# The down projection of a decoder layer as seven products of quadrants, with act split in two parts ahead and read back from DRAM

## The chip, the core and the metric

The kernel runs on one core of one Trainium2 chip. The metric is the device time of one execution in microseconds. The kernel before was run three times on the chip; the median counts, and one more execution was profiled.

## The reference

One decoder layer over 512 tokens of width 2048: an attention block with two groups of heads, then a gated feed-forward block of width 5632. All is float32. What the change touches is the last matrix product and what feeds it:

```python
h = rmsnorm(x, g_pre_ffn[l]) * (1.0 + sc_f) + sh_f
f = (jax.nn.silu(h @ w_gate[l]) * (h @ w_up[l])) @ w_down[l]
x = x + gt_f * rmsnorm(f, g_post_ffn[l])
```

Below, `act` is the 512 x 5632 matrix silu(gate) * up, and the down projection is act @ w_down, 512 x 5632 by 5632 x 2048. gt_f is a gate that comes from another product (w_ada), 2048 numbers, one for each output column.

## The kernel before

**Arithmetic.** A float32 product is made of three products of float32r parts: each factor is split in hi (a rounded copy, ACT) and lo (the rest, DVE), and `mm_x` (L281) issues hi*hi, lo*hi and hi*lo (L282 to L284) into one PSUM bank, 128 rows by 512 columns each. The weights are the moving operand, 512 columns; act or h is the stationary one, 128 columns.

**Steps.** The program is a list of steps. A step has one weight tile of 128 x 1024 (512 KB), which is two chunks of K by 512 columns. The main loop runs the steps in order and looks LA = 2 steps ahead: `do_hi` (L1533) lets ACT write w_hi of the step after next in the middle of a step, `do_lo` (L1542) lets DVE write w_lo at its end. Both have three buffers, so w_hi of step i+2 waits until TensorE is through with step i-1. Around this, events hang on a step: `start_ev`, `pe_ev`, `post_ev` (before do_lo), `post_end` (after it). Every engine works through its own instructions in the order in which this loop writes them, so the order of the events is the order on each engine. A transfer that SP starts waits in SP's order too, for a free buffer or for what it writes.

**Gate and up.** Steps F0 to F1 (32 steps) make the first group of 512 columns plainly. From F1 there are ten groups g of 28 steps each, with seven products of quadrants (Winograd's form: m1, P, Q, Y2, R, m2, T, four steps each, 12 matmuls a step). h's quadrants and their four sums E1 to E4 lie in SBUF in two parts; the sums of E are made during F0 to F1 (`e_sums` L1230, on DVE, with ACT's copy in the same event; `e_lo`). The sums of the weight quadrants are made in place: `w_load` (L1374) has SP fetch raw tiles; `w_sums` (L1386) adds to them by POOL's accumulating DMAs (P += B11 and P += B21 and R += B22) or by DVE (P += B22). A group's results are copied and combined out of PSUM (`s_copy`, `s_comb`), gated (`s_act1`, `s_act2a`, `s_act2b`) and transposed by TensorE (`act_tr`, L1250). ACT copies the transposed pieces to a stage buffer and its own queue writes them to a DRAM tile `act2d`, in float32. Five stage pieces of 128 x 1024 are shared among all this.

**Down.** Steps D0 on, 88 steps: four groups cg of 512 output columns, 22 steps of K each, 24 matmuls a step (four row blocks tb, two chunks of K, three part products). For every step SP fetches one weight tile and one act tile (512 KB each), ACT makes w_hi and the hi part of act (acthl, L967), DVE makes w_lo and the lo part of act (L971). So act is fetched and split four times over. 32 of the steps also carry a dot for gt_f on DVE (`ada_dot`, L226, a fetched 128 x 1024 tile each).

**End.** When a group cg is done, ACT squares its four banks with a running sum (L1475) and DVE multiplies them by the gain (L1479). The last three steps are held back and run row block by row block; after each block follow square, gain, `rstd` (L1141, L1145, and a power on POOL, L1146) and the outputs (L1488), which SP and ACT write to DRAM.

## Time and profile before

| what | value |
|---|---|
| runs | 2246.09, 2248.93, 2249.97 us; median 2248.93 |
| profiled execution, its own time | 2250.6 us |
| its span, first to last instruction | 2248.8 us |
| mean granted TensorE clock | 0.995 |
| one gate and up group (28 steps) | 78.33 us |
| down projection, first to last matmul start | 1759.1 to 2239.5 us |
| last matmul's start to the end | 9.3 us |
| DMA over the span | 524.02 MB, 233 GB/s |

A profile line of a group names line, engine, operation, output<-inputs, shape and count, then busy time, mean ns of one, and the idle time before it with what ended it. PE is TensorE's matmuls, PEld its weight loads. Matmuls overlap: the duration of one is longer than the distance from one to the next, so a rate is read from starts. A stretch of the windows view has busy time and count for PE, PEld, DVE, ACT and POOL, then the granted clock, the busy share of the 16 DMA engines, and GB/s.

### The profile page before, as it was taken

To read this page: it belongs to the slowest core of one execution; us is meant where nothing else is said; L and a number is where in the kernel's file an instruction comes from. 1 tells how busy PE (TensorE), PEld (TensorE's weight loads), DVE (VectorE), ACT (ScalarE), POOL (GpSimd) and SP (SyncE) were. 2 spreads that over 40 slices of the span, in tenths; PEclk is the share of its full clock that TensorE was granted. 3 is DMA by queue.
4 is the path that set the end of the run, shared out by engine and by line. 5 is a ranking of instruction groups with operands and counts; after the bars stand their busy time and mean duration, and the time that the engine had idled before them with its cause. 6 is when DMAs were issued, how large, how long until landed. Compare 5 with 4: busy or idle time off the path is not lost.

```text
span 2248.8 us, 27045 instructions
## 1 busy us (share of the span) xinstructions
PE 2214.3 (98%) x10012; PEld 1807.1 (80%) x10012; DVE 1471.7 (65%) x2117; ACT 1030.5 (46%) x1507; POOL 142.7 (6%) x156
## 2 busy tenths in 40 slices
PE   7999999999999999999999999999999999999998
PEld 6888777778887888777888888888888888888886
DVE  6987878776767676765566556556655666544445
ACT  5443344444435565544445445444544433343432
POOL 0000000000001000010111111011111000000000
PEclk9999999999999999999999999999999999999999
DMA  9786544556678787788877977897797788865564
GB/s 366 298 335 216 166 144 143 157 157 203 212 247 279 254 290 255 259 266 257 236 198 222 273 201 208 260 241 202 213 273 197 252 291 289 279 196 189 198 222 178
DMA packets 147845, 524.02 MB, mean 233 GB/s; under 512 B 16353, under 2 KB 27905, under 8 KB 141313
## 3 DMA queue, kind: packets, MB, share of 16 engines
q1 hardware_dynamic: 111696, 427.11, 54.6%
q0 software_dynamic: 17280, 62.92, 14.7%
q10 hardware_dynamic: 18736, 32.27, 4.6%
q8 instruction: 78, 1.28, 0.2%
q14 instruction: 55, 0.44, 0.1%
HBM read 488.14 MB, written 25.18 MB: 228 GB/s over the span
## 4 chain that ended last, share of the span: by engine, by line
PE 90%; DVE 4%; DMA 3%; issue 1%; ACT 1%; POOL 0%; SPq 0%; ACTq 0%; DVEq 0%; POOLq 0%
PE b L283 23%; PE b L284 23%; PE b L282 23%; PE b L277 5%; PE b L279 5%; PE b L278 5%; PE b L507 2%; DMA w_lent<-in_wgu 2%; DVE w_lo L1546 1%; PE b L545 1%; PE b L529 1%; PE b L1260 1%; PE b L500 1%; ACT w_hi L1537 1%; DMA w_raw<-in_wout 1%
## 5 line engine op out<-in xcount | busy, mean ns | idle before, releaser
L1546 DVE TENSOR_TENSOR w_lo<-w_raw,w_hi 128x1024 fp32r<-128x1024 f32 x264 | 321.9, 1222 | 280.3 <-ACT w_hi L1537 280.1
L1537 ACT ACTIVATE w_hi<-w_raw 128x1024 fp32r<-128x1024 f32 x264 | 278.3, 1057 | 424.0 <-PE b L284 333.2
L1546 DVE TENSOR_TENSOR w_lo<-raw,w_hi 128x1024 fp32r<-128x1024 f32 x189 | 230.5, 1223 | 186.6 <-ACT w_hi L1537 185.7
L282 PE MATMUL b<-w_hi,h 128*128 128x512 f32 x864 | 343.5, 398 | 1.9 <-ACT w_hi L1537 1.5
L283 PE MATMUL b<-w_lo,h 128*128 128x512 f32 x864 | 339.8, 393 | 5.0 <-DVE w_lo L1546 4.0
L284 PE MATMUL b<-w_hi,h 128*128 128x512 f32 x864 | 338.2, 391 | 0.0
L1537 ACT ACTIVATE w_hi<-raw 128x1024 fp32r<-128x1024 f32 x189 | 200.1, 1060 | 256.9 <-PE b L284 190.0
L284 PE MATMUL b<-w_hi,acthl 128*128 128x512 f32 x704 | 274.0, 389 | 0.4 <-DVE acthl L971 0.4
L282 PE MATMUL b<-w_hi,acthl 128*128 128x512 f32 x704 | 274.2, 389 | 0.0
L283 PE MATMUL b<-w_lo,acthl 128*128 128x512 f32 x704 | 273.9, 389 | 0.0
L283 PE MATMUL b<-w_lo,e 128*128 128x512 f32 x640 | 249.5, 390 | 2.2 <-DVE w_lo L1546 2.2
L282 PE MATMUL b<-w_hi,e 128*128 128x512 f32 x640 | 250.0, 391 | 0.3 <-ACT w_hi L1537 0.3
L284 PE MATMUL b<-w_hi,e 128*128 128x512 f32 x640 | 249.0, 389 | 0.0
L277 PE MATMUL b<-h,w_hi 128*128 128x512 f32 x512 | 212.9, 416 | 0.2 <-ACT h L257 0.2
L278 PE MATMUL b<-h,w_hi 128*128 128x512 f32 x512 | 200.5, 392 | 3.0 <-DVE h L273 3.0
L279 PE MATMUL b<-h,w_lo 128*128 128x512 f32 x512 | 201.3, 393 | 0.0
L283 PEld LDWEIGHTS b<-w_lo,h 128*128 128x128 f32 x864 | 163.1, 189 | 45.1 <-DVE w_lo L1546 11.7
L282 PEld LDWEIGHTS b<-w_hi,h 128*128 128x128 f32 x864 | 163.0, 189 | 40.2 <-issue 3.7
L284 PEld LDWEIGHTS b<-w_hi,h 128*128 128x128 f32 x864 | 163.0, 189 | 33.8
L1546 DVE TENSOR_TENSOR w_lo<-w_lent,w_hi 128x1024 fp32r<-128x1024 f32 x91 | 111.1, 1223 | 88.0 <-ACT w_hi L1537 87.7
L1537 ACT ACTIVATE w_hi<-w_lent 128x1024 fp32r<-128x1024 f32 x91 | 96.5, 1060 | 131.0 <-PE b L284 97.3
L284 PEld LDWEIGHTS b<-w_hi,acthl 128*128 128x128 f32 x704 | 132.2, 188 | 28.4 <-DVE acthl L971 0.8
(251 smaller groups left out, 3273.6 us busy)
## 6 DMA issues: line engine op xcount, KB each, us to landing
raw<-in_wgu SPq DMA_DIRECT2D x133, 512.0 KB, 8.8
w_raw<-in_adar SPq DMA_DIRECT2D x128, 512.0 KB, 4.3
w_raw<-in_win SPq DMA_DIRECT2D x107, 512.0 KB, 5.0
actf<-act2d SPq DMA_DIRECT2D x88, 512.0 KB, 4.7
w_raw<-in_wdown SPq DMA_DIRECT2D x88, 512.0 KB, 3.5
raw<-in_wgu POOLq DMA_DIRECT2D x82, 512.0 KB, 9.5
w_lent<-in_wgu SPq DMA_DIRECT2D x67, 512.0 KB, 8.7
w_raw<-in_wout SPq DMA_DIRECT2D x64, 512.0 KB, 4.9
```

The lines of the kernel that those rows point to most:

```text
L277: pe.matmul(ps, whi, ahi, start=start, stop=False, **kw)
L278: pe.matmul(ps, whi, alo, start=False, stop=False, **kw)
L279: pe.matmul(ps, wlo, ahi, start=False, stop=stop, **kw)
L282: pe.matmul(ps, ahi, whi, start=start, stop=False, **kw)
L283: pe.matmul(ps, ahi, wlo, start=False, stop=False, **kw)
L284: pe.matmul(ps, alo, whi, start=False, stop=stop, **kw)
L500: pe.matmul(sc[:, r], qk[:, i, qs], qk[:, i + 1, :N], start=True, stop=True)
L507: pe.matmul(sc[:, :N], qk[k, 2 * m, qs], qk[k, 2 * m + 1, :N], start=True, stop=True)
L529: pe.transpose(tr[:, j, :], misc["p"][:, n % 2, 128 * j:128 * j + 128], ident)
L545: pe.matmul(h["pv"][:, qb, :], d["pt"][:, o:o + 128], v[:, j, e], start=j == 0, stop=j == qb)
L1537: act.activation(hi, raw, AF.Copy)
L1546: dve.tensor_tensor(lo, raw, hi.bitcast(F), op=OP.subtract)
```

## The change

act is cut in four quadrants, two halves of rows and two halves of K (the even and the odd chunks of 128 of each group of 512, which is one of eleven steps j). w_down is cut in two halves of columns c, and each of these in quadrants of K and of 512 columns, which the host only lays out anew. For each c there are seven products of 11 steps with 12 matmuls: m1 (A11 by B11), P, R and Y2 (sums E1, E3, E4), then Q and m2 in turn, then T. Each sums its 11 steps in two PSUM banks; Q goes on in m1's banks and T in R's. The order of the steps and their transfers is fixed by lists:

```diff
+        DB = {"X": (0, 1), "Y": (4, 5), "Z": (2, 3), "W": (6, 7)}
+        DP = {"m1": ("A11", "X"), "P": ("E1", "Y"), "R": ("E3", "Z"), "Y2": ("E4", "W"),
+              "Q": ("E2", "X"), "m2": ("A12", "Y"), "T": ("A22", "Z")}
+        DUSE = {"m1": "C", "P": "C", "Q": "C", "T": "C", "R": "B12", "Y2": "B22", "m2": "B21"}
...
+            for j in range(2, 11):
+                seq += [("m1", j + 1)] * (j < 10) + [("P", j), ("R", j), ("Y2", j)]
+            for j in range(11):
+                seq += [("Q", j), ("m2", j)]
+            seq += [("T", j) for j in range(11)]
...
+                for k in range(2):
+                    ts_ = slice(128 * tb, 128 * tb + 128)
+                    mm_x(ps, hi4[:, k, :], lo4[:, k, :], at[:, 0, k, ts_], at[:, 1, k, ts_],
+                         first and k == 0, j == 10 and k == 1, skip_group_check=True)
```

Weight tile C holds B11 first; DVE adds B12, B22 and B21 to it in turn (and B22 to B12 for R), four sums of 128 x 1024 per j and c. The loads run 7 or 8 steps ahead, the act tiles and the tiles of the gt_f dots 5 steps:

```diff
+                dloads += [(dpos[c, "m1", j] - 7, dpos[c, "m1", j] - 4, c, "C", 0, j),
+                           (dpos[c, "P", j] - 8, dpos[c, "P", j] - 5, c, "B12", 1, j),
+                           (dpos[c, "R", j] - 8, dpos[c, "R", j] - 5, c, "B22", 3, j),
+                           (dpos[c, "m2", j] - 7, dpos[c, "m2", j] - 4, c, "B21", 2, j)]
+        dloads += [(i - 5, i - 2, 2, "dot", 0, i) for i in dots]
...
+        aloads = [(i - 5, *dseq[i - D0]) for i in range(D0, NSTEP)]
```

act's quadrants and sums are made while the next gate and up group runs, split in two parts there, and written to DRAM by SP (seven tiles of 512 KB a group, where 1 MB in float32 was written by ACT's queue before). A down step fetches one such tile and splits nothing but the weights:

```diff
+        def act_parts(g, at):
+
+            post_end[at].append(lambda: act_e(g, 0))
+            post_end[at + 1].append(lambda: act_e(g, 1))
+            for n, what in enumerate(("e0", "e1", "v0", "v1")):
+                post_end[at + 2 + 3 * n].append(lambda what=what: act_hi(g, what))
+                post_end[at + 3 + 3 * n].append(lambda what=what: act_lo(g, what))
+                start_ev[at + 4 + 3 * n].append(lambda what=what: act_out(g, what))
...
+            act_parts(g, b0 + 31)
...
-                    elif k - j == 7:
-                        pool.dma_start(rawt[g, "P", j], wgu[g, 1, j], accum_op=OP.add)
+                    elif k - j == 20:
+                        dve.tensor_tensor(rawt[g, "P", j], rawt[g, "P", j], rawt[g, "B21", j], op=OP.add)
...
+            post_end[at + 1].append(lambda j=j: e_hi(j))
+            post_end[at + 2].append(lambda j=j: e_lo(j))
```

act_e is four DVE sums of 128 x 512; act_hi is a copy on ACT into a new stage piece, act_lo a subtraction on DVE, act_out two transfers (hi, then lo), after which both pieces are free again. A sixth stage piece comes from a raw buffer. In the groups, raw buffers are fewer, and the first group fetches its third P tile at step F1 - 3 instead of F1 - 6. For h's sums, ACT's copy moves one step behind DVE's sums (e_hi).

At the end, the rows 0 to 255 are complete before T; their outputs come ahead of the last two steps (NLAST = 2), which then run for the two blocks of the lower rows:

```diff
-        NLAST = 3
+        NLAST = 2
...
+        for tb in range(2):
+            for q in range(2):
+                d_out(tb, 1024 * q, 1024)
+        for tb in range(2):
+            for i in last:
+                steps[i]["mm"](*hl[i], tb)
+            d_comb(1, 2, "R", OP.add, (tb,))
+            d_sq(1, 2, (tb,))
+            rstd(HF["dss", 2 + tb], 4)
+            d_gain(1, 2, (tb,))
+            for q in range(4):
+                d_out(2 + tb, 512 * q, 512)
```

TensorE has 9063 rows in order where it had 9327. Three places on the other engines follow. First ACT in one of the steady gate and up groups, before, from the copies of a group's first product (s1) to that of its second (y1); `stage` and `stageb` are stage pieces, DMAHW a transfer that SP or ACT started:

```order
L1289 ACTIVATE stage_6928<-b_10360 128x512
L1289 ACTIVATE stage_6928<-b_10369 128x512
L1537 ACTIVATE w_hi<-raw_7418 128x1024 [waits DMASW7_49,DVE_49,PE_49]
L1537 ACTIVATE w_hi<-w_lent 128x1024 [waits DVE_49,PE_49]
L1537 ACTIVATE w_hi<-raw_7683 128x1024 [waits DVE_49,PE_49]
L1537 ACTIVATE w_hi<-raw_7418 128x1024 [waits DVE_49,PE_49,Activation_49]
L1289 ACTIVATE stage_7304<-b_10448 128x512 [waits DMAHW7_49]
L1289 ACTIVATE stage_7304<-b_10457 128x512 [waits DMAHW0_49]
```

And after, from the copy of y1 (L1343) in step 8 of a group on; L1300 is act_hi, of e1 and then v0, L1343 further down the copy of u2:

```order
L1343 ACTIVATE stage_7304<-b_9975 128x512 [waits DMAHW6_49,DVE_49,Activation_49]
L1343 ACTIVATE stage_7304<-b_9984 128x512
L1300 ACTIVATE raw_7305<-stage_6928 128x1024 [waits DMAHW7_49]
L1704 ACTIVATE w_hi<-w_lent 128x1024 [waits DVE_49,PE_49,Activation_49]
L1704 ACTIVATE w_hi<-raw_7305 128x1024 [waits DMAHW1_49,PE_49,Activation_49]
L1704 ACTIVATE w_hi<-w_lent 128x1024 [waits DMAHW2_49,DVE_49,PE_49]
L1300 ACTIVATE raw_7305<-stageb 128x1024 [waits DMAHW2_49,DVE_49,Activation_49]
L1704 ACTIVATE w_hi<-raw_7680 128x1024 [waits DMAHW3_49,PE_49,Activation_49]
L1343 ACTIVATE stage_6928<-b_9887 128x512 [waits DMAHW3_49]
L1343 ACTIVATE stage_6928<-b_9896 128x512
L1704 ACTIVATE w_hi<-w_lent 128x1024 [waits DMAHW4_49,DVE_49,PE_49]
L1704 ACTIVATE w_hi<-raw_7681 128x1024 [waits DMASW4_49,DVE_49,PE_49]
```

Between two w_hi there are now ACT's splits, and those, like the copies, wait for a transfer that frees a stage piece; before, copies of y1 waited for act2d's writes alone.

Second, DVE in the down projection, before, two steps with a dot (L228) each:

```order
L971 TENSOR_TENSOR acthl<-actf,acthl 128x1024 [waits DMAHW1_49,PE_49,Activation_49]
L228 SCALAR_TENSOR_TENSOR w_raw,red<-w_raw,silu_back 128x1024 [waits DMAHW6_49,DVE_49]
L1546 TENSOR_TENSOR w_lo<-w_raw,w_hi 128x1024 [waits DMAHW0_49,Activation_49]
L971 TENSOR_TENSOR acthl<-actf,acthl 128x1024 [waits DMAHW4_49,PE_49,Activation_49]
L228 SCALAR_TENSOR_TENSOR w_raw,red<-w_raw,silu_back 128x1024 [waits DMAHW1_49,DVE_49]
L1546 TENSOR_TENSOR w_lo<-w_raw,w_hi 128x1024 [waits DMAHW3_49,Activation_49]
```

And after, four steps of Q and m2 in the first half, where L1713 makes w_lo, L1527 sums weight tiles (rawP, rawR, stage are buffers they lie in) and L228 is a dot:

```order
L1713 TENSOR_TENSOR w_lo<-rawR_13092,w_hi 128x1024 [waits DMAHW1_49,Activation_49]
L228 SCALAR_TENSOR_TENSOR stageb,red<-stageb,silu_back 128x1024 [waits DMAHW2_49]
L1527 TENSOR_TENSOR rawR_13093<-rawR_13093,raw_7681 128x1024
L1713 TENSOR_TENSOR w_lo<-rawP_13095,w_hi 128x1024 [waits Activation_49]
L1713 TENSOR_TENSOR w_lo<-rawP_13094,w_hi 128x1024 [waits DMAHW5_49,Activation_49]
L228 SCALAR_TENSOR_TENSOR stage_7304,red<-stage_7304,silu_back 128x1024 [waits DMAHW6_49]
L1527 TENSOR_TENSOR stage_6928<-stage_6928,rawR_13092 128x1024
L1713 TENSOR_TENSOR w_lo<-w_lent,w_hi 128x1024 [waits Activation_49]
```

The subtraction for act (L971) is gone; a pair of steps with 24 matmuls has two w_lo, a sum and a dot, where a step with 24 matmuls had one w_lo, one acthl and a dot.

Third, DVE at the end, before (du is the output tile, dss its sums, gtg the gain, x the residual), the last two row blocks:

```order
L1479 TENSOR_TENSOR du_13316<-b_15484,gtg_14444 128x512 [waits Activation_49]
L1141 TENSOR_REDUCE dss<-dss 128x1
L1145 TENSOR_SCALAR dss<-dss 128x1 [waits DVE_49]
L1488 SCALAR_TENSOR_TENSOR du_13316<-du_13316,dss,x_2_16008 128x1024 [waits DMAHW7_49,Pool_49]
L1488 SCALAR_TENSOR_TENSOR du_13316<-du_13316,dss,x_2_16008 128x1024
L1479 TENSOR_TENSOR du_13318<-b_15485,gtg_14444 128x512 [waits Activation_49]
L1141 TENSOR_REDUCE dss<-dss 128x1
L1145 TENSOR_SCALAR dss<-dss 128x1 [waits DVE_49]
L1488 SCALAR_TENSOR_TENSOR du_13318<-du_13318,dss,x_3_16076 128x512 [waits DMAHW3_49,Pool_49]
L1488 SCALAR_TENSOR_TENSOR du_13318<-du_13318,dss,x_3_16076 128x512 x3
```

And after, the two blocks of the lower rows, where L1612 adds T's bank, L1630 is the gain and L1654 the output:

```order
L1612 TENSOR_TENSOR du_14070<-du_14070,b_14806 128x512 [waits PE_49]
L1152 TENSOR_REDUCE dss<-dss 128x1 [waits Activation_49]
L1156 TENSOR_SCALAR dss<-dss 128x1 [waits DVE_49]
L1630 TENSOR_TENSOR du_14070<-du_14070,gtg_15892 128x512
L1654 SCALAR_TENSOR_TENSOR du_14070<-du_14070,dss,x_2_16070 128x512 [waits DMAHW5_49,Pool_49]
L1654 SCALAR_TENSOR_TENSOR du_14070<-du_14070,dss,x_2_16070 128x512
L1654 SCALAR_TENSOR_TENSOR du_14070<-du_14070,dss,x_2_16070 128x512 [waits DVE_49]
L1654 SCALAR_TENSOR_TENSOR du_14070<-du_14070,dss,x_2_16070 128x512
L1612 TENSOR_TENSOR du_14073<-du_14073,b_14815 128x512 [waits PE_49]
L1152 TENSOR_REDUCE dss<-dss 128x1 [waits Activation_49]
L1156 TENSOR_SCALAR dss<-dss 128x1 [waits DVE_49]
L1630 TENSOR_TENSOR du_14073<-du_14073,gtg_15892 128x512
```

A block had gain, sums and outputs; it now has a combination, sums that wait for ACT's square, the gain and four outputs, and the second block's combination stands behind the first one's outputs.

More of the change, by code (lines that the diff above doesn't have):

```diff
@@ L1262, in go_v @@
             def go_v():
                 stage.add(src())
-                p = stage.get()
-                v = v3(p, 4)
-                for n in range(2):
-                    act.activation(v[:, 2 * n:2 * n + 2, :], st[n], AF.Copy)
-                    act.dma_start(act2d[2 * g + n][:, :, 256 * half:256 * half + 256], v[:, 2 * n:2 * n + 2, :])
-                stage.add(p)
-            return go_pe, go_v
+                p = actv[g, f"v{half}"] = stage.get()
+                for f in range(2):
+                    act.activation(v3(p, 4)[:, 2 * f:2 * f + 2, :], st[f], AF.Copy)
@@ new lines, in body, with d_load @@
+        dloads.sort()
+        aloads = [(i - 5, *dseq[i - D0]) for i in range(D0, NSTEP)]
+        STAGE_RAW = ("P6", "T0", "SB", "P1")
+        XTAGS = ("P1", "P4", "R2", "R8")
+        def d_load(e):
+            while aloads and aloads[0][0] <= e:
+                c, name, j = aloads[0][1:]
+                p = apool.get()
+                assert p is not None, (e, aloads[0])
+                aloads.pop(0)
+                a_of[c, name, j] = p
+                v = p[1].rearrange("p (h k t) -> p h k t", h=2, k=2)
+                sync.dma_start(v, acts[ACOMBO[DP[name][0]], j])
+                atile[c, name, j] = v.bitcast(R)
+            while dloads and dloads[0][0] <= e:
+                at, end, c, n, q, j = dloads[0]
+                p = None
+                if c == 1 and n == "C":
+                    p = rawp.get([u for u in ("raw", "R10", "R11", "P2", "P5", *STAGE_RAW) if u not in XTAGS])
+                elif c == 1:
+                    p = rawp.get(XTAGS)
+                if p is None:
+                    p = rawp.get()
+                if p is None:
+                    assert end > e, (e, dloads[0], len(apool.free))
+                    break
+                dloads.pop(0)
+                draw_of[c, n, j] = p
+                draw[c, n, j] = p[1]
+                sync.dma_start(p[1], adar[dots[j]] if n == "dot" else wds[c, q, j])
@@ L1426, in body, with d_more @@
+        def d_more():
+            rawp.add(*stage.free)
+            stage.free = []
         w1 = wsteps[0, 1, 0, 0]
@@ new lines, in d_comb, with d_c12, d_sq @@
+        def d_comb(c, q, name, op, tbs=(0, 1)):
+            for tb in tbs:
+                dve.tensor_tensor(du(c, q, tb), du(c, q, tb), bank["d", c, name, tb], op=op)
+        def d_c12(c):
+            for tb in range(2):
+                dve.tensor_tensor(du(c, 1, tb), bank["d", c, "Y2", tb], du(c, 3, tb), op=OP.add)
+        sq = {}
+        def d_sq(c, q, tbs=(0, 1)):
+            if "t" not in sq:
+                sq["t"] = U("R7", [128, 4, 512], name="sq")
+            for tb in tbs:
+                t_, cg = 2 * (q // 2) + tb, 2 * c + q % 2
+                act.activation(sq["t"][:, tb, :], du(c, q, tb), AF.Square, accum_out=HF["dss", t_][:, cg:cg + 1])
```

278 lines of the change are left out of this document (169 added, 109 removed).

## The prediction

> **What bounds the kernel now.** I read the page first, then the down projection's matmuls, then the stages by windows, last the end of the program in order of time.
>
> The page, its first section and the chain by engine:
>
> ```profile
> span 2248.8 us, 27045 instructions
> PE 2214.3 (98%) x10012; PEld 1807.1 (80%) x10012; DVE 1471.7 (65%) x2117; ACT 1030.5 (46%) x1507; POOL 142.7 (6%) x156
> ...
> PE 90%; DVE 4%; DMA 3%; issue 1%; ACT 1%; POOL 0%; SPq 0%; ACTq 0%; DVEq 0%; POOLq 0%
> ```
>
> TensorE is the bound nearly everywhere. Whatever takes matmuls away without making TensorE wait shortens the run. The price of one matmul is not its 389 ns, though, because they overlap. The rows of the tile acthl (count, duration, first and last start) and two pairs of ACT's rows (start, duration, idle before):
>
> ```profile
> L282 PE MATMUL b<-w_hi,acthl x704: 387/389/476, 1759.1 to 2239.0; 128*128 128x512 f32 x176
> ...
> L284 PE MATMUL b<-w_hi,acthl x704: 388/389/500, 1759.7 to 2239.5; 128*128 128x512 f32 x176
> ```
> ```profile
> 2190.29 1.06 ACT L1537 ACTIVATE w_hi<-w_raw 128x1024 fp32r<-128x1024 f32 x1 [3.43 <-PE b L284]
> ...
> 2195.73 1.06 ACT L1537 ACTIVATE w_hi<-w_raw 128x1024 fp32r<-128x1024 f32 x1 [3.43 <-PE b L284]
> ```
> ```profile
> 1117.83 1.06 ACT L1537 ACTIVATE w_hi<-raw 128x1024 fp32r<-128x1024 f32 x1 [1.66 <-PE b L284]
> 1120.55 1.06 ACT L1537 ACTIVATE w_hi<-w_lent 128x1024 fp32r<-128x1024 f32 x1 [1.66 <-PE b L284]
> ```
>
> In the down projection one step (24 matmuls) takes 2195.73 - 2190.29 = 5.44 us, so a matmul costs 5.44/24 = 0.2267 us. The gate and up groups already run steps of 12 matmuls: 1120.55 - 1117.83 = 2.72 us, again 0.2267 each. The stage lasts 2239.5 - 1759.1 = 480.4 us, against 88 x 5.44 = 478.7: there is hardly a wait in it to win.
>
> **The change part by part.** *Matmuls.* Before: 88 steps of 24 = 2112. After: seven products x two column halves x 11 = 154 steps of 12 = 1848. That is 264 fewer, 264 x 0.2267 = **-59.8 us**, if every step keeps 2.72 us. The stage becomes 154 x 2.72 = 418.9 us.
>
> *What must keep up with 2.72 us.* Per step VectorE now makes one w_lo, and beside it sums of weight tiles (88) and gate dots (32), all 128x1024. Their price, a group and two neighbours on DVE:
>
> ```profile
> L1546 DVE TENSOR_TENSOR w_lo<-w_raw,w_hi 128x1024 fp32r<-128x1024 f32 x264 | 321.9, 1222 | 280.3 <-ACT w_hi L1537 280.1
> ```
> ```profile
> 1126.57 1.23 DVE L1305 TENSOR_TENSOR stage<-stage 128x1024 f32<-128x1024 f32 x1
> 1127.71 2.35 DVE L1546 TENSOR_TENSOR w_lo<-w_lent,w_hi 128x1024 fp32r<-128x1024 f32 x2
> ```
>
> Back to back such an operation takes 1127.71 - 1126.57 = 1.14 us. (154 + 88 + 32) x 1.14 = 312 us, and I estimate 30 us for combinations and gains: 342 of 418.9, 82%. The tightest stretches: Q and m2 in turn, two w_lo, a sum and a dot, 4.6 of 5.44 us; the T steps of the first half, 2.3 of 2.72. A w_lo starts 1.1 us into its step and is needed two steps on, after the first matmul: 5.44 + 0.23 - 1.06 - 1.22 = 3.4 us of slack. The first three T steps carry two pairs of PSUM combinations, 2 x 0.69 us each, and fall some 1.5 us behind; at the stage's start act_e0 and act_lo of the last group leave some 0.7 us. Both stay inside the slack on paper. ACT has one w_hi of 1.06 us per step and loses its acthl copy. Bounds 0 to +12; I take **+2**, nearest to the gate groups below, which run the same rhythm.
>
> *Gate and up groups.* The new act parts add four half sums, four ACT splits and four DVE subtractions per group, and P += B21 moves from POOL's accumulating DMA to DVE (four operations). Two of the steady groups (window, PE, PEld, DVE, ACT, POOL busy, clock, DMA share, GB/s):
>
> ```profile
> 1125.31:1203.64 78.33, 78.24 (x353) 64.64 (x352) 46.71 (x42) 37.58 (x43) 10.59 (x12) 1.00 0.84 228
> ...
> 1516.97:1595.30 78.33, 78.24 (x353) 64.66 (x353) 46.71 (x42) 37.58 (x44) 10.59 (x12) 1.00 0.82 226
> ```
>
> DVE has 46.7 of 78.33 us; it gets about 4 x 1.14 + 4 x 0.6 + 3.5 x 1.2 = 11 more, 58 (74%). A gain is excluded beyond 78.33 - 28 x 2.72 = 2.2 us, which also holds 16 transposes. The risk is not DVE's load but ACT: its split of e1 (and y1's copy just before) goes into pieces whose content SP is still writing to DRAM. By DVE's work in those steps, e0's lo is ready about 2.4 us into step 7 of a group and w_hi for step 11 must start by 0.8 us into step 10, so the write may take 5 us before TensorE waits. Nearest rows, the issues by time to landing and two windows there:
>
> ```profile
> raw<-in_wgu SPq DMA_DIRECT2D x133, 512.0 KB, 8.8
> ...
> act2d<-stage ACTq DMA_DIRECT2D x24, 256.0 KB, 3.7
> ...
> out<-du SPq DMA_DIRECT2D x6, 512.0 KB, 2.7
> ```
> ```profile
> 1144.48:1149.92 5.44, 5.44 (x25) 4.51 (x24) 3.28 (x3) 3.29 (x6) 0.00 (x0) 1.00 0.28 96
> ...
> 1149.92:1155.36 5.44, 5.44 (x25) 4.50 (x24) 5.33 (x6) 2.13 (x2) 0.97 (x2) 1.00 0.25 22
> ```
>
> Writes take 2.7 to 3.7 us, and the DMA engines are three quarters idle just there. I take +0.2 us per group, **+2** in all; bounds 0 and the slower rival below.
>
> *First group and start of the products.* Here the trace has a real stall:
>
> ```profile
> 951.70 0.80 PE L283 MATMUL b<-w_lo,h 128*128 128x512 f32 x1 [2.44 <-DVE w_lo L1546]
> ...
> 952.71 0.63 PE L282 MATMUL b<-w_hi,h 128*128 128x512 f32 x1
> ...
> 953.14 0.63 PE L283 MATMUL b<-w_lo,h 128*128 128x512 f32 x1
> ...
> 956.54 1.06 ACT L1243 ACTIVATE e<-stage 128x1024 fp32r<-128x1024 f32 x1 [4.98 <-DVE stage L1236]
> ```
> ```profile
> 950.00:960.00 10.00, 8.30 (x24) 6.63 (x25) 7.89 (x11) 3.57 (x4) 1.05 (x1) 0.66 0.71 191
> ```
>
> ACT waits for DVE's sums of e, the next w_hi is late, TensorE waits 2.44 us, and then some 14 matmuls come 0.43 us apart (953.14 - 952.71), twice the usual, at a granted clock of 0.66. A wait of this size thus costs itself plus 14 x 0.20 = 2.9 us. The Trainium skill, "TensorE: Matmul & The Clock Gate", Part 1, says the half clock comes after an idle window of about 3.4 us; here 2.44 us (after a shorter wait) was enough, so the row decides. The change puts ACT's split a step behind the sums: up to (44 - 24) x 0.2267 = 4.5 us less. Against it, the third load of P now comes three steps later, beside the first B11 loads: up to 1.3 + 2.9 = 4.2 us more, at 400 GB/s. I take **-1**.
>
> *The end.* Last matmul and what follows, in order of time:
>
> ```profile
> 2238.22 2.48 DVE L1488 SCALAR_TENSOR_TENSOR du<-du,dss,x 128x1024 f32<-128x1024 f32 x2 [0.73 <-POOL dss L1146]
> 2239.91 0.60 ACT L1475 ACTIVATE du<-b 128x512 f32<-128x512 f32 x1 [3.39 <-PE b L284]
> 2240.41 0.19 ACT L1475 ACTIVATION_READ_ACCUMULATOR du<-b 128x1 f32 x1
> 2240.63 0.69 DVE L1479 TENSOR_TENSOR du<-b,gtg 128x512 f32<-128x512 f32 x1
> 2241.24 0.14 DVE L1141 TENSOR_REDUCE dss<-dss 128x1 f32<-128x4 f32 x1
> 2241.42 0.15 DVE L1145 TENSOR_SCALAR dss<-dss 128x1 f32<-128x1 f32 x1
> 2241.72 0.55 POOL L1146 TENSOR_TENSOR dss<-dss,mhalf 128x1 f32<-128x1 f32 x1 [3.53 <-DVE dss L1145]
> 2242.30 2.74 DVE L1488 SCALAR_TENSOR_TENSOR du<-du,dss,x 128x512 f32<-128x512 f32 x4 [0.73 <-POOL dss L1146]
> ```
>
> Before, the end comes 2248.8 - (2239.5 + 0.39) = 8.9 us after the last matmul; 3.8 of it after DVE's last output. After, let s be the start of the last step run in order. DVE finishes its w_lo at s + 2.3 and then makes the four outputs of the upper rows (4 x 1.24) until s + 7.3. TensorE ends the first 128 lower rows at s + 5.4, the second at s + 8.2. For the first, the combination (0.69) starts at s + 7.3, square and sums end at 9.2, the power at 9.8, four outputs at 12.6. Only then, in DVE's order, comes the second: combination to 13.3, square 14.1, power 15.1, outputs 17.9, end s + 21.7. That is 13.4 us after the last matmul: **+4.4**. Ends: 0 if the upper outputs ran wholly ahead, +6 if x2 is late.
>
> **Sum.** -59.8 + 2 + 2 - 1 + 4.4 = -52.4. The profiled execution itself took 2250.6 us: 2198.2. The median of the three runs is 1.7 lower, 2248.9, so the forecast is **2196.5**; its own range, from the bounds, 2189 to 2204.
>
> **The rivals.** *The DMA engines pace the down projection.* It now moves 154 + 88 + 32 tiles of 0.524 MB and 4.2 MB of x2, 147.9 MB in 418.9 us, 353 GB/s. Rows of the queue and of windows:
>
> ```profile
> q1 hardware_dynamic: 111696, 427.11, 54.6%
> ```
> ```profile
> 20.00:40.00 20.00, 16.11 (x77) 12.80 (x76) 15.01 (x26) 9.89 (x17) 0.34 (x1) 0.85 1.02 419
> ...
> 60.00:80.00 20.00, 20.00 (x90) 16.58 (x89) 19.82 (x38) 9.67 (x12) 0.00 (x0) 1.00 0.99 372
> ...
> 2000.00:2050.00 50.00, 50.00 (x222) 41.41 (x221) 26.10 (x27) 21.44 (x28) 0.00 (x0) 1.00 0.59 196
> ```
>
> Against: 419 GB/s were moved in a full window. For: queue 1's mean is 427.11 MB in 54.6% of 2248.8, 348 GB/s at full share, and the down projection itself gives 196/0.59 = 332. At 348 the stage takes 425, +6, and in Q, m2 and T of the first half (53 tiles in 68 us, 409 GB/s) the lead of five steps is eaten; with three waits at 2.9 of half clock each, about +15: 2211. At 332 it takes 445, +27: 2223. Chance 0.17. The Trainium skill, "HBM Reference", Specifications, gives about 358 GB/s as a core's share; by that the stage would be 413 us, just hidden on the mean, and the 419 row shows that a core alone gets more.
>
> *VectorE falls behind in bursts.* If my 3.4 us of slack is short in two or three places per half, each wait costs 2 us: about +10, 2206. Speaking for it: 82% load in order. Chance 0.12.
>
> *Slower: ACT waits for the write of e0 in every group.* If those 512 KB land in 8.8 us, as the weight loads of this stage do on SP, instead of under 5, TensorE waits 3.9 us at step 11, pays 2.9 of half clock, and is late again when u2's copy waits for e1's write, some 3 more: about 10 per group, ten groups, +100 - 2: 2295. It decides from 52.4/10 = 5.2 us per group. Against it stand the idle windows and the write rows. Chance 0.06.
>
> *The saving is bigger* (no stall, the first group's 4.5 us won, no longer end): under 2189, chance 0.03. That the matmuls are not fewer can't be: the order of TensorE has 264 rows less.
>
> **How the numbers follow.** Forecast 0.62, the others as given. The range takes the forecast's own, the bursts and most of the DMA case: 2188 to 2215. No change to be measured (within 0.2%, 4.5 us, about what these runs can tell) would need a loss of about 50 us, between rivals: 0.01; slower 0.05, the rival's chance less a little for milder waits; faster 0.94.
>
> **What would show it.** Right: steps of 2.72 us on ACT through the down projection, about 419 us of it; groups of 78.3 to 78.8 us; 13 us after the last matmul. Wrong: TensorE waiting for a or raw tiles from DMA (first rival), for w_lo (second), ACT's splits waiting on DMA and groups over 80 us (third), or a clock under 1.00 after 1050 us.

## The result, and the profile after

The changed kernel takes 2194.65 us, the median of four runs (2193.78 to 2196.76), where the kernel before, run beside it, takes 2249.17: a ratio of 0.9761, 95% interval 0.9745 to 0.9778. The forecast was 2196.5. In a second comparison (five runs beside nine) it was 2197.41 against 2250.14, 0.9762 (0.9749 to 0.9775). The profiled execution took 2196.76 us, 53.8 less than that of before.

The page of the changed kernel, first section and chain by engine:

```profile
span 2195.0 us, 26915 instructions
PE 2152.4 (98%) x9748; PEld 1757.8 (80%) x9748; DVE 1668.9 (76%) x2333; ACT 1058.3 (48%) x1541; POOL 107.1 (5%) x116
...
PE 88%; DVE 5%; DMA 4%; ACT 1%; issue 1%; SPq 0%; POOL 0%; POOLq 0%; ACTq 0%; DVEq 0%
```

TensorE still holds the chain (88%, from 90), with 264 matmuls fewer; DVE's load went from 65% to 76%. The rows of the tile a, which takes acthl's place (first and last start), and what TensorE's idle time before them ended with:

```profile
L282 PE MATMUL b<-w_hi,a x616: 387/389/476, 1757.6 to 2180.6; 128*128 128x512 f32 x154
...
L284 PE MATMUL b<-w_hi,a x616: 388/389/402, 1758.1 to 2181.1; 128*128 128x512 f32 x154
...
  DVE w_lo L1713: 3.6, 6
...
  DMA a<-acts: 1.0, 2
```

The down projection lasts 2181.1 - 1757.6 = 423.5 us. Its waits are few: for w_lo at three places (the list counts a matmul and its weight load apart, which makes six), for act's tiles at two. Three of its windows (columns as in the table of the profile before):

```profile
1800.00:1850.00 50.00, 48.97 (x215) 39.79 (x214) 38.02 (x34) 19.11 (x18) 0.00 (x0) 1.00 1.03 411
...
1900.00:1950.00 50.00, 49.23 (x216) 40.12 (x215) 42.69 (x48) 22.74 (x30) 0.00 (x0) 1.00 1.00 389
1950.00:2000.00 50.00, 50.00 (x222) 41.39 (x221) 44.96 (x52) 21.42 (x26) 0.00 (x0) 1.00 0.97 370
```

The DMA engines, 0.70 busy over this stage before (0.59 in the window that the prediction shows), are 0.93 busy over it now and full from 1800 to 1850, at 411 GB/s, and that is where some 1.6 us go (215 matmuls where an undisturbed window has 222, 7 x 0.2267). Some 1.4 us more go from 1900 to 1950 (216 matmuls), where TensorE waits for w_lo at 1945.84 and at 1949.31, in the first T steps. DVE is busy 44.96 of the 50 us behind that. The end, on DVE in order of time, from the last three outputs of the upper rows:

```profile
2176.75 3.67 DVE L1654 SCALAR_TENSOR_TENSOR du<-du,dss,x 128x1024 f32<-128x1024 f32 x3
2180.34 0.68 DVE L1612 TENSOR_TENSOR du<-du,b 128x512 f32<-128x512 f32 x1
...
2183.19 2.74 DVE L1654 SCALAR_TENSOR_TENSOR du<-du,dss,x 128x512 f32<-128x512 f32 x4 [0.44 <-POOL dss L1157]
2185.85 0.68 DVE L1612 TENSOR_TENSOR du<-du,b 128x512 f32<-128x512 f32 x1
...
2188.71 2.74 DVE L1654 SCALAR_TENSOR_TENSOR du<-du,dss,x 128x512 f32<-128x512 f32 x4 [0.44 <-POOL dss L1157]
```

The second block's combination (2185.85) begins when the first block's outputs are done, 4.4 us after TensorE has finished for it. Where the time went, by stages of the two profiled executions; the first mark is ACT's sigmoid at the end of the first group with products (L1311, now L1365):

| stretch | before | after | difference | predicted |
|---|---|---|---|---|
| start to that sigmoid | 1054.5 | 1056.4 | +1.9 | -1 |
| from there to the down projection | 704.6 | 701.2 | -3.4 | +2 |
| down projection, first to last matmul start | 480.4 | 423.5 | -56.9 | -57.8 |
| last matmul's start to the end | 9.3 | 13.9 | +4.6 | +4.4 |
| span | 2248.8 | 2195.0 | -53.8 | -52.4 |

The two big terms came as forecast. The two small ones of the stages ahead both came with the wrong sign, and cancelled in part. That the total came so near is thus in part luck. Two rows of ACT show the second, that sigmoid in two groups in turn:

```profile
1134.37 1.06 ACT L1365 ACTIVATE stage<-b 128x512 f32<-128x512 f32 x2
...
1212.31 1.06 ACT L1365 ACTIVATE stage<-b 128x512 f32<-128x512 f32 x2
```

A group takes 77.94 us, where it took 78.33 and 78.5 was expected. In the first group the loss shows in short windows:

```profile
950.00:960.00 10.00, 10.00 (x46) 8.29 (x45) 8.66 (x14) 4.77 (x6) 1.93 (x2) 1.00 0.97 321
...
965.00:970.00 5.00, 2.27 (x10) 1.33 (x9) 1.65 (x3) 1.06 (x1) 1.74 (x2) 1.00 1.04 401
970.00:975.00 5.00, 4.63 (x14) 3.33 (x13) 2.71 (x5) 2.79 (x4) 0.00 (x0) 0.66 1.06 245
...
1010.00:1020.00 10.00, 6.08 (x22) 4.40 (x21) 3.84 (x4) 5.62 (x7) 0.87 (x1) 0.89 0.76 218
```

From 950 to 960, where the prediction saw a stall at half clock (24 matmuls), there are 46 now: that stall is gone. But from 965 to 975 there are 24 where 44 would fit, the second window at a clock of 0.66, with the DMA engines full. And from 1010 to 1020 there are 22. ACT's rows at these two places, and between them TensorE's at the first:

```profile
967.23 1.06 ACT L1704 ACTIVATE w_hi<-w_lent 128x1024 fp32r<-128x1024 f32 x1 [6.66 <-DMA w_lent<-in_wgu]
972.21 1.06 ACT L1704 ACTIVATE w_hi<-w_lent 128x1024 fp32r<-128x1024 f32 x1 [3.92 <-DMA w_lent<-in_wgu]
```
```profile
968.34 0.49 PE L282 MATMUL b<-w_hi,h 128*128 128x512 f32 x1 [1.97 <-ACT w_hi L1704]
...
969.60 0.50 PE L283 MATMUL b<-w_lo,h 128*128 128x512 f32 x1 [0.76 <-DVE w_lo L1713]
```
```profile
1011.87 1.09 ACT L1343 ACTIVATE stage<-b 128x512 f32<-128x512 f32 x2 [5.93 <-DMA acts<-stage]
1014.13 1.06 ACT L1300 ACTIVATE raw<-stageb 128x1024 fp32r<-128x1024 f32 x1 [1.17 <-DMA acts<-raw]
1015.09 2.94 ACT L1704 ACTIVATE w_hi<-raw 128x1024 fp32r<-128x1024 f32 x3
```

At the first, w_hi waits for weight tiles that are still on their way; ACT waits for such tiles at this place in the kernel before too (2.55 us at 968.56, 4.28 us at 973.91), so only a part of it is new. At the second, the copy of y1 waits 5.93 us for a write of act's parts to free its stage piece, and three w_hi come behind it in a row, late: that is the slower rival's mechanism, in this one group.

There is a third place, ahead of these. Relative to each other ACT's copy of e moved one step behind DVE's sums, but the copy kept its step: the sums and their loads moved one step forward. DVE at the first sum of e, before, and then after, with the matmul that waits:

```profile
921.12 1.23 DVE L1546 TENSOR_TENSOR w_lo<-w_raw,w_hi 128x1024 fp32r<-128x1024 f32 x1 [0.30 <-ACT w_hi L1537]
922.87 0.42 DVE L1233 TENSOR_TENSOR stage<-stage 128x256 f32<-128x256 f32 x1 [0.52 <-DMA w_raw<-in_wgu]
```
```profile
923.35 0.43 DVE L1244 TENSOR_TENSOR stage<-stage 128x256 f32<-128x256 f32 x1 [4.21 <-DMA w_raw<-in_wgu]
...
926.02 2.35 DVE L1713 TENSOR_TENSOR w_lo<-w_raw,w_hi 128x1024 fp32r<-128x1024 f32 x2
```
```profile
927.29 0.50 PE L283 MATMUL b<-w_lo,h 128*128 128x512 f32 x1 [2.12 <-DVE w_lo L1713]
```

Before, w_lo came ahead of the sum; now it stands behind a sum that waits 4.21 us for a transfer, and TensorE waits 2.12 us for it.

In the steady groups the slower rival's wait does not decide. The second write of e0 is issued at 1155.61 and the split of e1 that needs its piece starts at 1159.04, 3.4 us later, so the write lands inside the 5 us that the prediction allowed:

```profile
1155.61 0.38 SPq L1313 DMA_DIRECT2D acts<-raw  x1
```
```profile
1159.04 1.06 ACT L1300 ACTIVATE raw<-stageb 128x1024 fp32r<-128x1024 f32 x1 [0.96 <-DMA acts<-raw]
...
1171.35 1.09 ACT L1343 ACTIVATE stageb<-b 128x512 f32<-128x512 f32 x2 [3.36 <-DMA acts<-stageb]
```

Not every write is that quick: the copy of u2 (1171.35) waits 3.36 us for a write that was issued at 1163.47, 7.9 us earlier. TensorE does not wait there either.

### The profile page after: what moved, and what is told of

The parts are those of the page before. It is cut to its first block, busy times and chain, and to the rows that moved or that the text cites. A ratio compares the mean times of both kernels' runs of the same rounds, so it can differ in the third digit from the quotient of the medians.

```text
span 2195.0 us, 26915 instructions
## 1 busy us (share of the span) xinstructions
PE 2152.4 (98%) x9748; PEld 1757.8 (80%) x9748; DVE 1668.9 (76%) x2333; ACT 1058.3 (48%) x1541; POOL 107.1 (5%) x116
## 4 chain that ended last, share of the span: by engine, by line
PE 88%; DVE 5%; DMA 4%; ACT 1%; issue 1%; SPq 0%; POOL 0%; POOLq 0%; ACTq 0%; DVEq 0%
PE b L283 22%; PE b L282 22%; PE b L284 22%; PE b L277 6%; PE b L279 5%; PE b L278 5%; PE b L507 2%; DVE w_lo L1713 2%; DMA a<-acts 1%; PE b L545 1%; DMA raw<-in_wgu 1%; PE b L1276 1%; PE b L500 1%; PE b L529 1%; ACT w_hi L1704 1%
## 5 line engine op out<-in xcount | busy, mean ns | idle before, releaser
L1713 DVE TENSOR_TENSOR w_lo<-raw,w_hi 128x1024 fp32r<-128x1024 f32 x232 | 282.7, 1222 | 140.9 <-ACT w_hi L1704 140.7
L1704 ACT ACTIVATE w_hi<-raw 128x1024 fp32r<-128x1024 f32 x232 | 245.6, 1060 | 291.7 <-PE b L284 216.8
L1713 DVE TENSOR_TENSOR w_lo<-w_raw,w_hi 128x1024 fp32r<-128x1024 f32 x176 | 214.2, 1221 | 61.3 <-ACT w_hi L1704 61.1
L1704 ACT ACTIVATE w_hi<-w_raw 128x1024 fp32r<-128x1024 f32 x176 | 185.2, 1055 | 142.7 <-PE b L284 58.3
L283 PE MATMUL b<-w_lo,a 128*128 128x512 f32 x616 | 240.0, 390 | 1.1 <-DVE w_lo L1713 1.1
L282 PE MATMUL b<-w_hi,a 128*128 128x512 f32 x616 | 240.1, 390 | 1.0 <-DMA a<-acts 1.0
L284 PE MATMUL b<-w_hi,a 128*128 128x512 f32 x616 | 239.7, 389 | 0.0
L1704 ACT ACTIVATE w_hi<-w_lent 128x1024 fp32r<-128x1024 f32 x128 | 135.7, 1061 | 165.8 <-PE b L284 125.2
L1713 DVE TENSOR_TENSOR w_lo<-w_lent,w_hi 128x1024 fp32r<-128x1024 f32 x128 | 156.3, 1223 | 76.7 <-ACT w_hi L1704 76.7
L282 PEld LDWEIGHTS b<-w_hi,e 128*128 128x128 f32 x640 | 120.5, 188 | 28.5 <-ACT w_hi L1704 3.6
```

The lines of the kernel that those rows point to most:

```text
L282: pe.matmul(ps, ahi, whi, start=start, stop=False, **kw)
L283: pe.matmul(ps, ahi, wlo, start=False, stop=False, **kw)
L284: pe.matmul(ps, alo, whi, start=False, stop=stop, **kw)
L1704: act.activation(hi, raw, AF.Copy)
L1713: dve.tensor_tensor(lo, raw, hi.bitcast(F), op=OP.subtract)
```

## The experiments

The theory: the products save 264 matmuls at their full price; the groups gained because eight transposes of each moved from step 28 to 27, an edit that the description of the change does not name; the first group lost by waits for transfers; nothing else matters. The rivals say that the gain of the groups comes from other edits there, or that some limit of the down projection (DMA, DVE) costs more than its waits show.

**The order of two writes.** The lo part goes to DRAM ahead of the hi part, so the stage pieces come free in the other order.

```diff
-            for part, w in enumerate((what + "h", what)):
+            for part, w in ((1, what), (0, what + "h")):
```

> SP writes the lo part of each act piece to DRAM ahead of its hi part, so that the first piece to come free waits for VectorE's subtraction. This puts the slower rival of the prediction to the test. Theory A (the groups stand close to the edge: ACT's next copy now waits until about 2 us into step 9 instead of running early in step 8, w_hi for step 11 comes late): groups of 79 to 82 us and the kernel 10 to 40 us longer, with TensorE waiting for w_hi and half clock. Theory B (two steps of lookahead still cover it): ACT waits longer, groups stay at 77.95 to 78.1, the kernel within 3 us.

Measured (one run): 2251.23 us, span 2249.5; the down projection starts at 1812.5, 54.9 later. TensorE's and ACT's waits from 1040 to 1740, and one group by windows:

```profile
PE b L282 <- ACT w_hi L1704: 17.3, 8, 3.2
```
```profile
ACT stage L1300 <- DMA acts<-stage: 47.4, 12, 8.2
ACT stageb L1300 <- DMA acts<-stageb: 40.5, 8, 6.6
```
```profile
1145.38:1228.88 83.50, 80.25 (x354) 65.54 (x353) 56.62 (x54) 40.48 (x48) 6.98 (x8) 0.98 0.75 221
```

The same 354 matmuls now take 83.5 us. ACT's split waits up to 8.2 us (the changed kernel: 1.2 at most), the next w_hi stands behind it in ACT's order, and TensorE waits up to 3.2 us and then loses clock. Nine groups (from the first such sigmoid to the down projection) take 751.5 us instead of 701.2, 5.6 us more each; 4.1 us of the 54.9 had arisen by 921, ahead of all groups. That ate the whole gain, as the prediction's point of 5.2 us a group had it. So the wait that the slower rival describes is real, and the order of two transfers decides whether TensorE sees it. Here the first write of e0 starts 21.2 us behind the sigmoid (1166.62) instead of 15.5 (1149.88), because it stands behind DVE's subtraction; the rival had the write land late, and its price of about 10 us a group was almost twice what this costs.

**The first group one step earlier.** In the other groups act's parts begin in step 3 of the next group, for the first one in step 4.

```diff
-        for hf, at in ((0, F0 + 32), (1, F0 + 36)):
+        for hf, at in ((0, F0 + 32), (1, F0 + 35)):
...
-        act_parts(0, F0 + 36)
+        act_parts(0, F0 + 35)
```

> The act parts of the first gate and up group are made one step earlier, in the place that all later groups have. Theory A (ACT waits for the write that frees a stage piece, and only in the first group TensorE pays for it, 3.2 us of waiting and a stretch at half clock): the wait at about 1011 us goes, the kernel is 4 to 5 us shorter, about 2190. Theory B (the loss there comes from the late weight tiles of the first group, not from the stage pieces): no change, within 1 us.

Measured: 2192.92 us (2191.26 to 2193.84), ratio 0.9744 (0.9727 to 0.976); the down projection starts at 1753.9, 3.7 earlier, and lasts as long. From 1000 to 1020 there are 79 matmuls, not 66. The copy of y1 still waits 6.1 us, but a step ahead in the program, so TensorE's waits for w_hi from 940 to 1040 fall from 5.1 to 2.5 us. The ratios' intervals of the two kernels overlap; it is the trace that shows the gain.

**The sums of e back in their old place.** The loads and DVE's sums go back one step, into the event of ACT's copy, which keeps its step.

```diff
-            at = F0 + 16 + 5 * j // 2
+            at = F0 + 17 + 5 * j // 2
...
-            post_end[at + 1].append(lambda j=j: e_hi(j))
-            post_end[at + 2].append(lambda j=j: e_lo(j))
+            post_end[at].append(lambda j=j: e_hi(j))
+            post_end[at + 1].append(lambda j=j: e_lo(j))
```

> ACT's copy of h's sums goes back into the same event as VectorE's sums, as in the kernel before, one step later in the program than now. Theory A (moving the copy behind the sums spared TensorE a wait, as the prediction had it): ACT waits longer for the sums, and the stretch from 900 to 985 us loses 2 to 5 us more. Theory B (the copy still waits for the sums after the change and its place matters little): within 1.5 us either way.

Measured (one run): 2201.81 us, span 2199.9, the down projection from 1762.3, 4.7 later. TensorE has its 2.4 us wait for w_lo back. But the 4.7 us are not the edit's: two rows of ACT, the w_hi just ahead of the first sum of e and the ninth behind it, stand in the changed kernel at

```profile
916.82 1.06 ACT L1704 ACTIVATE w_hi<-w_raw 128x1024 fp32r<-128x1024 f32 x1 [0.67 <-PE b L284]
...
944.91 1.04 ACT L1704 ACTIVATE w_hi<-w_raw 128x1024 fp32r<-128x1024 f32 x1
```

and in this run at 920.33 and 950.27. So 3.5 us were lost ahead of the edited place, and between the two rows it takes 29.9 us instead of 28.1. The edit is worth some 2 to 3 us (the table below): the stall at 950 less the new wait at 927.29.

**The transposes, alone in the kernel before, and undone in the changed one.** In the kernel before, eight transposes of each group move from step 28 to 27, and to banks 6 and 7:

```diff
-            a, b = act_tr(g, 0, lambda g=g: ffn[g, "s1"], (4, 5))
-            pe_ev[b0 + 28].append((0, a))
-            post_ev[b0 + 28].append(b)
+            a, b = act_tr(g, 0, lambda g=g: ffn[g, "s1"], (6, 7))
+            pe_ev[b0 + 27].append((0, a))
+            post_ev[b0 + 27].append(b)
```

> The kernel before with one move out of the change: in the ten groups the eight transposes of act's first half stand in step 27 of a group instead of step 28, in banks 6 and 7. Theory A, that the groups became shorter by this alone because the transposes fill the time in which TensorE waited about 0.5 us for w_lo, says a period of about 77.9 us instead of 78.33 and 4 us off the whole, about 2245.5 us, 0.998 of the kernel before. Theory B, that the shorter groups come from the other edits there (P += B21 off POOL's queue, act's writes off ACT's queue), says 78.3 us per group and no change of the time.

And in the changed kernel they go back to step 28 (27 to 28 in the same two lines):

> The transposes of the first half of a group's act go back from step 27 to step 28, as in the kernel before; all else is the changed kernel. Theory A (the groups became 0.38 us shorter because eight transposes now stand ahead of the matmuls that waited 0.5 us for w_lo): the group is 78.3 us again, the kernel about 3.5 us longer, 2198. Theory B (the gain per group comes from the accumulating DMA that was dropped, or from ACT's queue having no writes to start): the group stays at 77.95 and the kernel at 2194.7.

Measured: 2247.0 us (2243.59 to 2250.52) against 2249.19, ratio 0.9987 (0.9979 to 0.9996), span 2245.4; undone in the changed kernel 2200.45 (2199.41 to 2203.85), 0.9781 (0.9767 to 0.9796). A group by the sigmoid, first in the kernel before with the move:

```profile
1131.78 1.06 ACT L1311 ACTIVATE stage<-b 128x512 f32<-128x512 f32 x2
...
1209.73 1.06 ACT L1311 ACTIVATE stage<-b 128x512 f32<-128x512 f32 x2
```

That is 77.95 us without any of the other edits; undone, it is 78.37 (1132.87 and 1211.24). What went is TensorE's wait in its weight loads from 1060 to 1740, in the kernel before and in the changed one with the move undone:

```profile
PEld b L283 <- DVE w_lo L1546: 4.2, 9, 0.5
```
```profile
PEld b L283 <- DVE w_lo L1713: 4.9, 9, 0.6
```

Once per group TensorE waited about 0.5 us for w_lo; with the transposes ahead of that matmul the wait is filled with work that had to be done anyway. Before with the move has no such row. So some 4 us of the 54 belong to this move and not to the products (nine groups: 704.6 us without it and 700.4 with it in the kernel before, 701.2 with it and 705.4 without it in the changed one; the medians differ by 2.2 us in the kernel before and by 3.0 to 5.8 us in the changed one).

**More transfers in the down projection.** Each step of the first half also fetches 256 KB that nothing uses.

```diff
+            if D0 <= e < D0 + 77:
+                if "x" not in extra:
+                    extra["x"] = U("R5", [128, 4, 512], name="extra")
+                sync.dma_start(extra["x"][:, e % 4, :], t["wout"][e % 4, e % 8][:, 0:512])
```

> In each of the 77 steps of the down projection's first half SP fetches 256 KB more that nothing reads, 20.2 MB in 209 us. That half then needs 74.4 + 20.2 = 94.6 MB, 452 GB/s at the pace of TensorE. Theory A (the stage is close to the DMA engines' limit, the 411 GB/s seen in one window at full share being that limit): the first half takes 94.6/0.411 = 230 us instead of 211, the kernel is about 20 us longer, and TensorE waits for DMA or w_hi. Theory B (there is room left, 450 GB/s can be had): within 3 us.

Measured (one run): 2223.46 us; the down projection lasts 450.3, 26.8 more. The waits at the tile a, with the time to landing, and two windows:

```profile
  DMA a<-acts: 20.6, 28
...
DMA to landing us min/median/max: 3.2/8.4/10.8
```
```profile
1800.00:1850.00 50.00, 44.13 (x185) 33.83 (x184) 32.62 (x29) 16.75 (x16) 0.00 (x0) 1.00 1.03 406
...
1950.00:2000.00 50.00, 42.54 (x173) 31.22 (x172) 40.14 (x52) 19.94 (x29) 0.00 (x0) 1.00 1.03 404
```

Full engines move 404 to 406 GB/s here. The Trainium skill, "HBM Reference", Specifications, gives about 358 GB/s as a core's share and says that a core alone gets well above it; these rows agree with the second half. At 405 the stage's 147.9 MB need 365 of 423.5 us: the mean has room (less by the engines' busy share, 0.93, than by the bytes), and the stretch around 1800 has none. The added 77 x 0.262 = 20 MB would take 50 us at that rate; 27 of them showed, so by this estimate the half with them had some 23 us of room in all.

**The gate's dots without DVE's work.** The tiles are still fetched.

```diff
-                ada_use(*dots[e])(draw[2, "dot", e])
+                n_, ch_, hf_ = dots[e]
+                dve.tensor_scalar(red[:, 2 + n_, hf_, ch_:ch_ + 1], draw[2, "dot", e][:, 0:1], 1.0, None, op0=OP.mult)
```

> VectorE doesn't make the 32 dots for gt_f (one element of each tile is copied instead); their tiles are still fetched. The gate of the output is thus not computed. Theory A (the small waits of TensorE for w_lo in T, 2.4 us in all, are VectorE's load of 82 percent coming in bursts): those waits go, the kernel is 1.5 to 2.5 us shorter, and VectorE falls from 84 to about 75 percent there. Theory B (the waits come from tiles that land late): no change, within 0.5 us in the length of the down projection (423.5 us).

Measured (one run): 2195.88 us; the down projection lasts 422.3, 1.2 less, and TensorE waits for w_lo at one place instead of three (1.2 us in that list instead of 3.6). The dots' share of DVE's bursts costs about a microsecond.

**Fewer matmuls in T.** The T steps leave out one of their three part products, 88 matmuls in all, 20 us at full price.

```diff
+                    if name == "T":
+                        pe.matmul(ps, at[:, 0, k, ts_], hi4[:, k, :], start=False, stop=False, skip_group_check=True)
+                        pe.matmul(ps, at[:, 0, k, ts_], lo4[:, k, :], start=False, stop=j == 10 and k == 1,
+                                  skip_group_check=True)
+                        continue
```

> In the 22 steps of T the part product of act's lo part is left out, so a T step has 8 matmuls in place of 12: 88 matmuls less. Theory A (only TensorE's count matters): 88 x 0.2267 = 19.9 us shorter, about 2175. Theory B (VectorE is the next bound: in the first half's T steps, 1.81 us long, it has w_lo and a dot, 2.3 us, and two pairs of combinations): in the first half only 4 to 5 us of 10 are won, the second half's 10 in full, so 14 to 15 us shorter, about 2180, with TensorE waiting for w_lo.

Measured (one run): 2196.8 us, span 2194.7: nothing gained, where theory B expected 14 to 15 us. The down projection is 4.3 us shorter (1758.6 to 2177.8), but what follows it is 3.0 us longer: the first combination of the end starts at 2179.98, hardly sooner than in the changed kernel (2180.34). Two windows, in T of the first and of the second half, and the waits at the tile a:

```profile
1960.00:1980.00 20.00, 17.39 (x69) 12.39 (x69) 20.00 (x25) 7.95 (x12) 0.00 (x0) 1.00 1.03 411
...
2160.00:2185.00 25.00, 15.73 (x63) 11.04 (x61) 23.67 (x35) 7.33 (x12) 2.59 (x3) 0.96 0.66 266
```
```profile
  DVE w_lo L1718: 28.1, 33
```

DVE is busy all 20 us, and TensorE waits for it 33 times by this list (14 matmuls, 19 weight loads). In T, DVE is the next bound, right behind TensorE. The prediction's 2.3 of 2.72 us holds for a w_lo and a dot alone. The first T steps carry three pairs of combinations (1938.75, 1943.36 and 1946.84 in the changed kernel), not two, and a sum of weight tiles; those of the second half carry the gains. It hides here because three part products are just long enough.

**The end.** The outputs of the upper rows run in T6 to T8, and the second block's combination comes ahead of most of the first block's outputs.

```diff
+            for q in range(2):
+                post_end[dpos[1, "T", 6] + (2 * tb + q) // 2 + (2 * tb + q) % 2].append(
+                    lambda tb=tb, q=q: d_out(tb, 1024 * q, 1024))
...
-        for tb in range(2):
-            for q in range(2):
-                d_out(tb, 1024 * q, 1024)
...
             d_sq(1, 2, (tb,))
+            if tb == 1:
+                for q in range(2):
+                    d_out(2, 512 * q, 512)
             rstd(HF["dss", 2 + tb], 4)
             d_gain(1, 2, (tb,))
-            for q in range(4):
-                d_out(2 + tb, 512 * q, 512)
+        for q in range(2, 4):
+            d_out(2, 512 * q, 512)
+        for q in range(4):
+            d_out(3, 512 * q, 512)
```

> The outputs of the upper rows are made during the last T steps, and at the end the second lower block's combination comes ahead of the first block's outputs. Theory A (the end is VectorE's order: 4 outputs ahead, then block after block): the first combination starts right after its matmuls, the end shrinks from 13.6 to about 11 us after the last matmul, the kernel is 2.6 us shorter, about 2192. Theory B (the end is set by the writes to DRAM behind the outputs, which start together): no change, within 0.5 us.

Measured: 2193.62 us (2192.09 to 2196.17), ratio 0.975 (0.9735 to 0.9764), span 2191.3. DVE at the end, the two combinations and the last outputs:

```profile
2178.20 0.69 DVE L1612 TENSOR_TENSOR du<-du,b 128x512 f32<-128x512 f32 x1 [0.32 <-PE b L284]
...
2180.92 0.69 DVE L1612 TENSOR_TENSOR du<-du,b 128x512 f32<-128x512 f32 x1 [0.29 <-PE b L284]
...
2183.70 4.06 DVE L1654 SCALAR_TENSOR_TENSOR du<-du,dss,x 128x512 f32<-128x512 f32 x6
```

Both combinations now start 0.3 us after TensorE releases them. From the last matmul's start (2180.5) to the end it is 10.8 us, 3.1 less. TensorE's waits for w_lo in this stage are 5.8 us in that list instead of 3.6, since the outputs compete with it in T. The time alone can't tell this version from the changed kernel (the intervals overlap); the end of the trace can.

**Both edits together.** The first group's parts a step earlier, and the end as above.

> Two edits that each helped by themselves, put together: the first group's parts of act one step earlier, and the outputs of the upper rows in the T steps with the second lower block's combination ahead of the first block's outputs. They lie at different places of the program, so theory A says that their savings in span add: 2195.0 - 3.5 - 3.7, a span of about 2187.8 us and a time of about 2189 us, 0.973 of the kernel before. Theory B, that the earlier outputs' VectorE work makes the last T steps late and that this cancels (TensorE waited 5.8 us for w_lo there), says no more than the first edit alone, 2192 to 2193 us.

Measured: 2190.16 us (2186.58 to 2193.79), ratio 0.9742 (0.9728 to 0.9755), span 2184.8. Its matmuls at the tile a:

```profile
L282 PE MATMUL b<-w_hi,a x616: 387/389/476, 1749.5 to 2173.5; 128*128 128x512 f32 x154
```

The down projection starts 8.1 us sooner than in the changed kernel, 4.4 sooner than with the first edit alone, though the programs are alike up to there: 1.3 of the 4.4 us had arisen by 916, 1.8 come from the first group and 1.4 from the groups behind it (the table below). To get a fair distance, both once more on one chip:

> The changed kernel once more, unaltered, on the same chip and in the same rounds as the version with both edits, to have a fair distance between the two. Both theories expect about 2195 us, 0.976 of the kernel before, as in its first comparison.

> The two edits together (first group's parts of act one step earlier, outputs of the upper rows in the T steps), beside the unaltered changed kernel on the same chip. Theory A, that both savings are real and add, expects it 5 to 7 us shorter than the changed kernel, about 2189 us, 0.9735 of the kernel before, with intervals that hardly overlap. Theory B, that its first runs were short by chance of the early stages, whose start moves by 2 to 4 us between kernels that are alike there, expects no more than 2 to 3 us between them.

Measured: 2197.41 us (2195.28 to 2198.75, five runs) and 2192.35 (2187.5 to 2193.94, four runs), 0.9762 and 0.9739 (0.9725 to 0.9752). The version is 5.1 us shorter by the medians, no run of one within the runs of the other; the ratios' intervals overlap by 0.0003. That is the lower end of what the two savings would add up to.

**The stages ahead, side by side.** Profiled executions, in us; the marks are the two rows of ACT above, the first group's sigmoid and the first matmul of the down projection. The first column is a time, the others are stretches.

| kernel | w_hi ahead of the sums of e | to the ninth w_hi | to the sigmoid | to the down projection |
|---|---|---|---|---|
| before | 917.3 | 30.4 | 106.8 | 704.6 |
| before, transposes in step 27 | 918.2 | 29.7 | 105.9 | 700.4 |
| changed | 916.8 | 28.1 | 111.5 | 701.2 |
| changed, once more | 918.9 | 27.6 | 112.2 | 700.7 |
| changed, sums of e back | 920.3 | 29.9 | 111.0 | 701.0 |
| changed, transposes in step 28 | 917.3 | 27.1 | 110.1 | 705.4 |
| changed, two writes swapped | 921.0 | 26.8 | 113.3 | 751.5 |
| changed, first group earlier | 916.8 | 27.3 | 107.5 | 702.4 |
| both edits, first and second time | 915.6, 917.2 | 27.3, 27.1 | 105.7, 105.7 | 701.0, 701.0 |

Each column answers one question. Ahead of the products the executions differ by 5.4 us, and no edit shown here explains it. The edit at e is worth some 2 to 3 us. The first group is some 5 us longer in the changed kernel, and as short as before when its act parts come a step earlier. The transposes are worth 4 us in nine groups.

## Why the prediction was right, and where it was not

**Matmuls.** Right, as mechanism and as size: 264 at 0.2267 us. Steps kept 2.72 us nearly everywhere; the stage took 423.5 against 418.9 without a wait.

**Waits in the down projection.** +2 was forecast, +2.9 measured (4.6 us of waits, less 1.7 before). Their places were the window with full DMA engines from 1800 on, and DVE in T of the first half (and once, at 2156.89, of the second). The slack did not hold everywhere: in T the working had a pair of combinations and a sum too few, and the room in DMA was worked out as a mean.

**Gate and up groups.** The step that failed is the sum for a group: it had +0.2 us, and each gave -0.38. The estimate of ACT's waits was right where it was made (e0's writes land in 3.4 of 5 us, and TensorE waits for none of the writes in steady groups). What was missed is that the move of eight transposes takes away a wait of 0.5 us per group; the prediction does not mention the move, and only bounds a gain at 2.2 us. The kernel before with nothing but this move gives the same 77.95 us.

**First group and start of the products.** -1 was forecast, +1.9 came: -0.5 from the spread ahead of the products, -2.3 at the sums of e, +4.7 from there to the sigmoid. The prediction's stall at 951.70 is read rightly, but the row of ACT that it shows (956.54) starts after it. The copy of e that held it up is this one:

```profile
946.70 1.06 ACT L1243 ACTIVATE e<-stage 128x1024 fp32r<-128x1024 f32 x1 [4.08 <-DVE stage L1236]
```

The gain of up to 4.5 us was there, but the same edit makes the wait at 927.29, and 2 to 3 us are left. The step that failed is the term of the loss. It had 4.2 us at most, for late loads of P, and nothing for the act parts of the first group, which begin a step later than in the others. Those are what cost the time: with them a step earlier the stretch to the sigmoid is 105.7 to 107.5 us, where the kernel before has 106.8 and the changed one 111.5. The late tiles at 968.34 (TensorE waits 1.97 us, then runs at half clock) come late in that version too (1.31 us at 966.86). The matmul that waits has h as its stationary operand, so the tile is not P's but one that loads beside it. Whether these loads are late because the third P load or the whole load order came later was not tried.

**The end.** Right: 13.4 us after the last matmul ends, 13.6 measured (2195.0 - 2181.05 - 0.39 = 13.56), by the cause that was named, DVE's order: with the order altered it is 3.1 us less.

**The rivals.** DMA as the pace: not in this kernel; the rows of 332 and 348 GB/s it was built on were no ceiling, since 404 to 411 are moved in full windows. DVE in bursts: 1.2 us without the dots. The slower one: swapping two writes brings about the wait that it names. The 5.2 us from which it decides were right; its price was not, 5.6 us a group where it had about 10. What delays ACT's split in that run is first a later start of the writes; the landing of e0's write in 8.8 us, which the rival assumed, no run shows.

## What to carry to other kernels

Where TensorE is the bound, a saving of matmuls can be counted at their distance from start to start, but the engines behind it must then be counted per step and with every operation that stands in those steps, not as a mean over the stage. Where a buffer comes free by a transfer, the order in which the transfers are issued can decide the wait: here swapping two writes cost 5.6 us in each of nine groups. Where an edit's worth is smaller than what the stages ahead of it vary by, measure it between two marks around the edited place: the start of the down projection said 4.7 us for the edit at e, the marks said 2 to 3. And work that some engine must do anyway belongs just ahead of an instruction that waits, as the transposes showed.
